# A two-layer encoder on one core: later loads of job blocks, sums written over the raw blocks, six part buffers, A22's low part by VectorE, and the mixer's jobs in another order

## The chip, the cores and the metric

The kernel runs on one core of a Trainium2 chip. The metric is the device time of one execution in microseconds, the median of several runs. The engines are named as in the profile: PE is TensorE's matmul, PEld its weight load, DVE is VectorE, ACT is ScalarE, POOL is GpSimd and SP is SyncE, which here only issues loads.

## The reference

The input is one sequence of 512 tokens with 1024 channels, and each of two layers does this (cut):

```python
h = rmsnorm(x, g_ffn1[l]);  x = x + 0.5 * (silu(h @ w1_a) * (h @ w3_a)) @ w2_a     # 1024 -> 2816 -> 1024
h = rmsnorm(x, g_mix[l]);   p = h @ w_in[l]                                        # fourier|B|C|v|pool|3 gates
y_f = fourier_mix(p_f, w_fourier);  y_c = (B * conv3(C * v)) @ w_conv_out
y_p = pool_scale * per_group(centred_mean(u) - u)                                  # windows 2, 4, 8, 16
x = x + (sig(g_f) * y_f + sig(g_c) * y_c + sig(g_p) * y_p) @ w_o
h = rmsnorm(x, g_ffn2[l]);  x = x + 0.5 * (silu(h @ w1_b) * (h @ w3_b)) @ w2_b
```

After the layers comes a last rmsnorm. All of it is float32.

## The kernel before

**Products.** Activations lie with channels on the 128 partitions and the 512 tokens along the row. A matrix product keeps float32's precision by splitting both operands into a high part (a cast to fp32r) and a low part (the operand minus its high part): `mm` issues three matmuls, high by high (L367), high by low (L368) and low by high (L369).

**Jobs.** The pair w3 and w1 of an f-block of 128 channels (or two blocks of w_in in the mixer) is one *job* in Strassen's form in Winograd's variant. Its weights are cut in four blocks A11, A12, A21, A22, its activations in four quarters, and seven products M1 to M7 take the place of eight. One product is four `mm` of 128x256, so 12 matmuls, and a job has 84. `run` issues per job M1, M5, then M4 of the job before, M6, M3 of the job before, M2, M7. M1, M6, M7 and M4 of one job add up in one PSUM bank; after M1, M6 and M7 ScalarE copies the running sum to a tile sM (`kept`, L536), so M4 can't begin until the copy after M7 has been made. VectorE adds these copies into the two outputs a and b; in a feed-forward stage it then multiplies b by silu(a) (L442 `b<-b,a`), ScalarE casts the high part gh (L354), and VectorE makes the low part gl. The plain tiles, 128x512 matmuls, are w2, w_o, the small maps and the first f-blocks of each feed-forward stage: three (`LEAD`), four in the first stage. `lead` does those while the norm's factor and the split operands n of the jobs (`operands`, four calls a stage) are still being made.

**The stream of weights.** `Weights` loads blocks from DRAM by SP (L193) into 3 buffers `raw` (A11 and A12, 512 KB), 2 of `z` (A21, 256 KB) and 2 of `w22` (A22, 256 KB). Four splitting steps per job fill buffers of parts: *raw* splits the raw block, *sums* makes z + w22 (L236) and that less A11 (L237) and splits both, *rest* makes A11|A12 less the z block (L243, into a tile s34 of its own) and splits it, and *last* splits A22 for M4. Splitting comes in two ways. `parts` casts the high part on ScalarE (L199) and subtracts on VectorE (L200). `added_parts` writes minus the block on ScalarE (L212), lets POOL issue a DMA that adds the block from DRAM to it once more (L213), and casts the high part (L214); VectorE has no part in it. *raw* and *last* use this way, so the low part of A22 costs ScalarE one pass and POOL one DMA.

**What sets the order.** A planner logs every tile and product in the order in which PE needs them with a rough time, and subtracts from it a number per kind of step (`AHEAD`, in planner's microseconds). A step is written into the program once PE's place has come that near, if its buffers are free. After that the framework's scheduler puts each engine's instructions in their order; at run time each engine works its list strictly in order, and waits at an instruction whose inputs or whose buffer aren't there. SP too issues one load after the other, and a load waits for the release of its buffer. A w22 buffer is free when the steps *sums* and *last* have read it.

## Time and profile before

| | us |
|---|---|
| median of 3 runs | 2104.84 (2100.64 to 2105.34) |
| the profiled execution | 2107.87 |
| its span in the trace | 2106.1 |
| PE busy in the span | 2049.9 |
| DVE busy | 1288.2 |
| ACT busy | 1214.6 |
| POOL busy | 383.4 |

The mean granted clock of TensorE was 0.993 of 2.4 GHz in the profiled execution. The run goes in this order: the first feed-forward stage with its lead (0 to about 398 us of the trace), the mixer of the first layer (398 to 662), the second feed-forward stage (662 to 1036) and the third (1036 to 1430), the mixer of the second layer (1430 to 1700), and the last stage. A matmul's record shows a longer time than the next one's distance, because matmuls overlap: the pace is the distance of their starts. Idle time before an instruction stands in brackets behind it, with what ended it.

### The profile page before, as it was taken

What the parts mean: (1) busy time and instruction counts of PE and PEld (TensorE: products, weight loads), DVE (VectorE), ACT (ScalarE), POOL (GpSimd) and SP (SyncE); (2) the same over time, 40 slices, a digit from 0 to 9 for tenths busy, and PEclk for the clock granted to TensorE, in tenths of its full rate; (3) what the DMA queues carried; (4) which work ended last, traced back from release to release, by engine and by line L of the source; (5) the groups of instructions that cost most, each with busy time, mean ns of one, the idle gap of its engine ahead of it and who ended that gap; (6) DMA issues with size and microseconds to landing.
All of it is one profiled execution on the core that took longest, in us unless ns stands there. A gap on an engine that the chain in (4) does not pass through costs nothing. (4 is left out here: it accounts for less than half of the span.)

```text
span 2106.1 us, 34329 instructions
## 1 busy us (share of the span) xinstructions
PE 2049.9 (97%) x13590; PEld 1870.8 (89%) x13590; DVE 1288.2 (61%) x1868; ACT 1214.6 (58%) x1963; POOL 383.4 (18%) x452
## 2 busy tenths in 40 slices
PE   8899999999999999999999999999999999999998
PEld 6798998899988899899889899988999888988996
DVE  4863674698876575366366546638888656653653
ACT  5762764776655665366466446548666556644652
POOL 3310111211221310011231001122122123100100
PEclk9999999999999999999999999999999999999999
DMA  8763774877665776477567557658777567744751
GB/s 232 164 178 95 173 177 130 171 169 175 159 161 150 154 188 163 105 172 182 137 135 188 145 125 165 181 124 162 175 174 180 141 156 151 181 141 113 173 152 54
DMA packets 121555, 329.03 MB, mean 156 GB/s; under 512 B 13489, under 2 KB 15153, under 8 KB 121393
## 3 DMA queue, kind: packets, MB, share of 16 engines
q0 software_dynamic: 45360, 121.28, 34.2%
q1 hardware_dynamic: 75888, 205.31, 30.0%
q8 instruction: 106, 1.74, 0.3%
q14 instruction: 57, 0.46, 0.1%
q10 hardware_dynamic: 144, 0.24, 0.0%
HBM read 312.10 MB, written 2.10 MB: 149 GB/s over the span
## 5 line engine op out<-in xcount | busy, mean ns | idle before, releaser
L368 PE MATMUL ps<-n,parth 128*128 128x256 f32 x2760 | 777.9, 282 | 9.2 <-DMA n<-t 4.6
L369 PE MATMUL ps<-n,partl 128*128 128x256 f32 x2760 | 777.2, 282 | 8.2 <-DMA partl<-weights 5.4
L367 PE MATMUL ps<-n,parth 128*128 128x256 f32 x2760 | 777.2, 282 | 7.7 <-ACT n L484 2.4
L368 PEld LDWEIGHTS ps<-n,parth 128*128 128x128 f32 x2760 | 522.2, 189 | 12.7 <-DMA n<-t 5.8
L367 PEld LDWEIGHTS ps<-n,parth 128*128 128x128 f32 x2760 | 521.8, 189 | 12.2 <-ACT n L484 2.8
L369 PEld LDWEIGHTS ps<-n,partl 128*128 128x128 f32 x2760 | 522.0, 189 | 10.0 <-DMA partl<-weights 6.5
L213 POOL DMA_DIRECT2D partl<-weights x152 | 133.9, 881 | 631.3 <-ACT partl L212 523.0
L367 PE MATMUL ps<-gh,parth 128*128 128x512 f32 x616 | 242.9, 394 | 0.0
L368 PE MATMUL ps<-gl,parth 128*128 128x512 f32 x616 | 242.6, 394 | 0.0
L369 PE MATMUL ps<-gh,partl 128*128 128x512 f32 x616 | 242.5, 394 | 0.0
L200 DVE TENSOR_TENSOR partl<-z,parth 128x1024 fp32r<-128x1024 f32 x115 | 142.8, 1242 | 153.0 <-ACT parth L199 151.3
L213 POOL DMA_DIRECT2D part22l<-weights x115 | 101.1, 879 | 726.3 <-ACT a L662 418.6
L199 ACT CAST parth<-raw 128x1024 fp32r<-128x1024 f32 (+3 forms) x127 | 125.2, 986 | 174.4 <-PE ps L368 123.2
L200 DVE TENSOR_TENSOR partl<-raw,parth 128x1024 fp32r<-128x1024 f32 (+3 forms) x127 | 152.1, 1203 | 113.5 <-ACT parth L199 113.1
L214 ACT CAST parth<-raw 128x1024 fp32r<-128x1024 f32 (+1 forms) x152 | 157.8, 1038 | 90.6 <-PE ps L368 60.7
L212 ACT ACTIVATE partl<-raw 128x1024 fp32r<-128x1024 f32 (+1 forms) x152 | 158.7, 1044 | 14.6 <-DMA raw<-weights 10.3
L200 DVE TENSOR_TENSOR partl<-s,parth 128x1024 fp32r<-128x1024 f32 x115 | 145.8, 1268 | 34.2 <-ACT parth L199 34.0
L236 DVE TENSOR_TENSOR z<-z,w 128x512 f32<-128x512 f32 x115 | 80.2, 697 | 127.1 <-DMA w<-weights 116.1
L199 ACT CAST parth<-z 128x1024 fp32r<-128x1024 f32 x115 | 120.4, 1047 | 51.6 <-PE ps L368 48.9
L536 ACT COPY sM<-ps 128x256 f32<-128x256 f32 x345 | 121.5, 370 | 47.6 <-PE ps L369 46.0
L367 PE MATMUL ps<-n,part22h 128*128 128x256 f32 x460 | 134.0, 291 | 11.1 <-ACT sM L536 10.3
L243 DVE TENSOR_TENSOR s<-raw,z 128x1024 f32<-128x1024 f32 x115 | 141.5, 1231 | 1.0
(184 smaller groups left out, 3539.9 us busy)
## 6 DMA issues: line engine op xcount, KB each, us to landing
raw<-weights SPq DMA_DIRECT2D x258, 512.0 KB, 4.1
partl<-weights POOLq DMA_DIRECT2D x145, 512.0 KB, 6.2
z<-weights SPq DMA_DIRECT2D x115, 256.0 KB, 4.1
w<-weights SPq DMA_DIRECT2D x115, 256.0 KB, 4.1
part22l<-weights POOLq DMA_DIRECT2D x115, 256.0 KB, 5.3
n<-t POOLq DMA_DIRECT2D x48, 256.0 KB, 5.4
x<-x_t SPq DMA_DIRECT2D x8, 256.0 KB, 5.4
raw<-weights SPq DMA_DIRECT2D x11, 128.0 KB, 3.5
```

The source lines that it names most:

```text
L199: self.nc.scalar.copy(hi[:, :w], src)
L200: self.tail.append((self.t, self.made, lambda: self.nc.vector.tensor_tensor(out=lo[:, :w], in0=src, in1=hi[:, :w].bitcast(F32), op=ALU.sub ...
L212: self.nc.scalar.activation(lo[:, :w], src, AF.Copy, scale=-1.0)
L213: self.nc.gpsimd.dma_start(lo[:, :w], self.source(key), accum_op=ALU.add)
L214: self.nc.scalar.copy(hi[:, :w], src)
L236: v.tensor_tensor(out=z[:, 2 * S :], in0=z[:, :S], in1=w22, op=ALU.add)
L243: v.tensor_tensor(out=s34, in0=raws.pop(("first", key))[:, : 2 * S], in1=raws.pop(("third", key))[:, : 2 * S], op=ALU.subtract,)
L367: nc.tensor.matmul(ps, ah, bh, start=start, stop=False, skip_group_check=more)
L368: nc.tensor.matmul(ps, ah, bl, start=False, stop=False, skip_group_check=more)
L369: nc.tensor.matmul(ps, al, bh, start=False, stop=stop, skip_group_check=more)
L536: nc.scalar.copy(b["s" + q], ps)
```

## The change

- **Plan.** Loads of A11|A12 begin 21 (before 24) planner's microseconds ahead, loads of A21 and A22 17 (19); the steps *raw*, *sums* and *rest* are made one earlier (14, 9, 8), *last* 8 ahead instead of 12. Six part buffers for five; the tile s34 is gone, and UNITS, the activation tiles, fall from 50 to 48.
- ***rest*** writes its difference over the raw block, which so stays taken until the split has read it.
- ***last*** uses `parts`: 115 ScalarE passes (L212, 128x512) and 115 accumulating DMAs of 256 KB go, and 115 subtractions of 128x512 on VectorE come.
- **operands** makes two separate tiles of its two inputs, writes them contiguously, and gives M1 the 256-wide pair whose casts are first; three small subtractions become four.
- **The first lead** asks for the norm's factor at its step 12 (15), for the spread at 14 (17), for the four operands at 15, 17, 20, 23 (18, 21, 25, 28).
- **HALF** is 10 for 11: the first stretch of jobs of a feed-forward stage is one shorter, the second one longer.
- **Mixer.** After the Fourier gates come pool, conv, b and p jobs interleaved; before, two pool jobs stood among the Fourier gates. In the pool gates the sum onto yf moves from POOL to VectorE (16 additions of 128x512), and the tiles z and y of the convolution come from the activations' pool.

```diff
-LEAD, HALF = 3, 11
+LEAD, HALF = 3, 10
-    AHEAD = {... "load1": 24.0, "load2": 19.0, "raw": 13.0, "sums": 8.0, "rest": 7.0, "last": 12.0}
+    AHEAD = {... "load1": 21.0, "load2": 17.0, "raw": 14.0, "sums": 9.0, "rest": 8.0, "last": 8.0}
-    BUFS = {"raw": 3, "z": 2, "w22": 2, "s34": 1, "part": 5, "part22": 1}
+    BUFS = {"raw": 3, "z": 2, "w22": 2, "part": 6, "part22": 1}
...
-            s34 = self.tile_of("s34", 2 * S)
-            v.tensor_tensor(
-                out=s34, in0=raws.pop(("first", key))[:, : 2 * S], in1=raws.pop(("third", key))[:, : 2 * S],
...
+            raw = raws.pop(("first", key))[:, : 2 * S]
+            v.tensor_tensor(out=raw, in0=raw, in1=raws.pop(("third", key))[:, : 2 * S], op=ALU.subtract)
+            self.ready["rest", key] = self.parts(raw)
...
-            self.ready["last", key] = self.added_parts(raws.pop(("fourth", key)), ("fourth", key), S, "part22")
+            self.ready["last", key] = self.parts(raws.pop(("fourth", key)), S, "part22")
...
-        place = {"M1": (0, 0), "M2": (0, 1), "M3": (3, 0), "M5": (1, 0), "M7": (1, 1), "M6": (2, 0), "M4": (2, 1)}
+        place = {"M1": (3, 0), "M2": (0, 0), "M3": (0, 1), "M5": (1, 0), "M7": (1, 1), "M6": (2, 0), "M4": (2, 1)}
...
-            at = {"factor": 15, "spread": 17, "operands": (18, 21, 25, 28), "done": (24, 26, 29, 99)}
+            at = {"factor": 12, "spread": 14, "operands": (15, 17, 20, 23), "done": (26, 29, 99)}
...
-            if i in (1, 2):
-                job("pool", 2 * i - 2, OFF_P + (2 * i - 2) * P, OFF_P + (2 * i - 1) * P)
...
+        for do, i in (
+            (pool_in, 0), (conv_in, 0), (pool_in, 2), (pool_gate, 0), (conv_in, 1), (conv_gate, 0), (pool_gate, 1),
+            (conv_in, 2), (pool_gate, 2), (conv_in, 3), (conv_gate, 2), (pool_gate, 3),
+        ):
+            do(i)
...
-                ptt(yf[m], yf[m], s, ALU.add)
+                tt(yf[m], yf[m], s, ALU.add)
```

How the change moves instructions shows at three places. The first is VectorE's list in the steady part of a feed-forward stage, one job's round; the numbers behind the names are buffers of single allocations. Before:

```order
L236 TENSOR_TENSOR z_13249<-z_13249,w22_13251 128x512
L442 TENSOR_TENSOR b_13194<-b_13194,a_13193 128x512
L442 TENSOR_TENSOR b_13327<-ps_13286,sM1_13211 128x256
L237 TENSOR_TENSOR z_13249<-z_13249,raw_13155 128x512
L200 TENSOR_TENSOR partl_13380<-s34_13377,parth_13379 128x1024
L442 TENSOR_TENSOR gl_13310<-b_13194,gh_13309 128x512
L442 TENSOR_TENSOR a_13326<-ps_13214,sM7_13323 128x256
L243 TENSOR_TENSOR s34_13510<-raw_13155,z_13249 128x1024
L200 TENSOR_TENSOR partl_13405<-z_13249,parth_13404 128x1024
L442 TENSOR_TENSOR b_13327<-ps_13214,sM6_13265 128x256
```

Now the same round on VectorE, with L228, L229, L235 and L192 for L236, L237, L243 and L200:

```order
L192 TENSOR_TENSOR part22l_13392<-w22_13132,part22h_13391 128x512
L431 TENSOR_TENSOR b_13316<-ps_13207,sM6_13255 128x256
L431 TENSOR_TENSOR b_13316<-b_13316,a_13315 128x512
L228 TENSOR_TENSOR z_13389<-z_13389,w22_13394 128x512
L431 TENSOR_TENSOR b_13447<-ps_13408,sM1_13335 128x256
L192 TENSOR_TENSOR partl_13472<-raw_13190,parth_13471 128x1024
L431 TENSOR_TENSOR gl_13430<-b_13316,gh_13429 128x512
L431 TENSOR_TENSOR a_13446<-ps_13338,sM7_13443 128x256
L229 TENSOR_TENSOR z_13389<-z_13389,raw_13321 128x512
L235 TENSOR_TENSOR raw_13321<-raw_13321,z_13389 128x1024
L192 TENSOR_TENSOR partl_13490<-z_13389,parth_13489 128x1024
```

The product b by a stood behind the addition that reads w22 and now stands ahead of it. New is part22l three places ahead of that addition, and the two hang together: the slot of w22_13132, which part22l reads last, is the one into which w22_13394 is loaded.

The second place is SP's list of loads in the same stretch, before:

```order
L193 DMA raw_13288<-weights 128x1024
L193 DMA w22_13118<-weights 128x512
L193 DMA z_13249<-weights 128x512
L193 DMA raw_13421<-weights 128x1024
L193 DMA w22_13251<-weights 128x512
L193 DMA z_13382<-weights 128x512
```

And now:

```order
L185 DMA raw_13059<-weights 128x1024
L185 DMA z_13127<-weights 128x512
L185 DMA w22_13001<-weights 128x512
L185 DMA raw_13190<-weights 128x1024
L185 DMA z_13258<-weights 128x512
L185 DMA w22_13132<-weights 128x512
```

The load of w22 stood right behind a raw block of 512 KB; now the 256 KB of z stand between.

The third place is VectorE's list in the first lead, from the norm's spread on, before:

```order
L470 SCALAR_TENSOR_TENSOR s34_381<-x0_86,cst_70,rstd_373 128x2x256
L470 SCALAR_TENSOR_TENSOR s34_381<-x1_87,cst_70,rstd_373 128x512
L442 TENSOR_TENSOR t_382<-s34_381 128x512
L237 TENSOR_TENSOR z_527<-z_527,raw_423 128x512
L442 TENSOR_TENSOR t_383<-s34_381,t_382 128x256
```

And now:

```order
L457 SCALAR_TENSOR_TENSOR t_357<-x0_86,cst_70,rstd_345 128x512
L457 SCALAR_TENSOR_TENSOR t_358<-x1_87,cst_70,rstd_345 128x512
L431 TENSOR_TENSOR t_359<-t_357 128x256
L431 TENSOR_TENSOR t_359<-t_358,t_357 128x256
L431 TENSOR_TENSOR t_360<-t_358,t_359 128x256
L431 TENSOR_TENSOR t_360<-t_358,t_360 128x256
L229 TENSOR_TENSOR z_560<-z_560,raw_493 128x512
```

The subtraction that reads the raw block stood in the middle of the first operand's four steps, and now stands behind all of them.

## Rows read from the trace of the kernel before

**Rows 1.** The page, busy time, share of the span and instructions of PE

```profile
PE 2049.9 (97%) x13590; PEld 1870.8 (89%) x13590; DVE 1288.2 (61%) x1868; ACT 1214.6 (58%) x1963; POOL 383.4 (18%) x452
```

**Rows 2.** Waits of PEld, whole run: us in total, times, longest us

```profile
PEld ps L367 <- ACT sM L536: 18.6, 35, 3.1
PEld ps L369 <- DMA partl<-weights: 7.7, 6, 2.6
PEld ps L368 <- DMA n<-t: 5.8, 6, 1.6
...
PEld ps L369 <- DMA part22l<-weights: 4.0, 5, 1.9
```

**Rows 3.** Timeline of PE, 26 matmuls apart: start us, us, engine, instruction

```profile
1809.79 0.28 PE L369 MATMUL ps<-n,partl 128*128 128x256 f32 x1
...
1812.86 0.28 PE L368 MATMUL ps<-n,parth 128*128 128x256 f32 x1
```

**Rows 4.** Chain of waits, 1955 to 1986 us: start us, us, what

```profile
1959.13 4.18 DMA w<-weights
...
1969.33 4.25 DMA w<-weights
```

**Rows 5.** Timeline of SP's queue, just ahead of the load in Rows 4

```profile
1958.70 0.33 SPq L193 DMA_DIRECT2D raw<-weights  x1
```

**Rows 6.** The tile w, 808 to 815 us, one load, issued at 811.9

```profile
DMA to landing us min/median/max: 2.7/2.7/2.7
```

**Rows 7.** Timeline of DVE, one job's round

```profile
1964.61 0.42 DVE L442 TENSOR_TENSOR b<-ps,sM 128x256 f32<-128x256 f32 x1
1964.95 0.68 DVE L237 TENSOR_TENSOR z<-z,raw 128x512 f32<-128x512 f32 x1
1965.55 1.22 DVE L200 TENSOR_TENSOR partl<-s,parth 128x1024 fp32r<-128x1024 f32 x1
1966.68 0.69 DVE L442 TENSOR_TENSOR gl<-b,gh 128x512 fp32r<-128x512 f32 x1
```

**Rows 8.** Groups of DVE by form: busy us, mean ns | idle before, releasers

```profile
L236 DVE TENSOR_TENSOR z<-z,w 128x512 f32<-128x512 f32 x115 | 80.2, 697 | 127.1 <-DMA w<-weights 116.1 <-issue 8.1 <-DMA z<-weights 2.8
```

**Rows 9.** Timeline of DVE, one of the longer of these waits

```profile
1817.04 0.69 DVE L236 TENSOR_TENSOR z<-z,w 128x512 f32<-128x512 f32 x1 [4.48 <-DMA w<-weights]
```

**Rows 10.** Busy time by windows: us, PE, PEld, DVE, ACT, POOL, PEclk, DMA share, GB/s

```profile
64.80:71.60 6.80, 4.24 (x18) 3.95 (x19) 6.09 (x9) 3.50 (x7) 3.96 (x4) 0.50 0.90 153
...
1819.20:1822.60 3.40, 3.29 (x15) 3.29 (x16) 3.27 (x5) 1.24 (x4) 0.00 (x0) 0.51 0.03 6
```

**Rows 11.** Busy time by windows, the first mixer

```profile
398.00:662.00 264.00, 257.62 (x1963) 247.21 (x1962) 209.68 (x339) 178.98 (x305) 54.73 (x78) 0.99 0.71 167
```

**Rows 12.** Timeline of POOL in the first mixer

```profile
594.81 1.29 POOL L445 TENSOR_TENSOR yf<-yf,a 128x512 f32<-128x512 f32 x1 [0.65 <-DVE a L968]
596.04 0.89 POOL L213 DMA_DIRECT2D partl<-weights  x1
598.37 2.19 POOL L445 TENSOR_TENSOR yf<-yf,b 128x512 f32<-128x512 f32 x1 [1.43 <-DVE b L968]
```

**Rows 13.** Timeline of DVE at the same place

```profile
599.66 1.98 DVE L200 TENSOR_TENSOR partl<-raw,parth 128x1024 fp32r<-128x1024 f32 x1
```

**Rows 14.** Timeline of PE, first lead, eight matmuls apart

```profile
36.74 0.40 PE L367 MATMUL ps<-hh,parth 128*128 128x512 f32 x1
...
38.60 0.39 PE L369 MATMUL ps<-hh,partl 128*128 128x512 f32 x1
```

**Rows 15.** Timeline of DVE, first lead

```profile
49.20 0.69 DVE L237 TENSOR_TENSOR z<-z,raw 128x512 f32<-128x512 f32 x1 [4.09 <-DMA raw<-weights]
```

**Rows 16.** Timeline of PE, the first jobs

```profile
64.80 0.57 PE L367 MATMUL ps<-n,parth 128*128 128x256 f32 x1 [2.05 <-ACT n L484]
67.93 0.58 PE L368 MATMUL ps<-n,parth 128*128 128x256 f32 x1 [2.56 <-DVE n L442]
```

**Rows 17.** DMA queues on the page: packets, MB, share of 16 engines; q0 is POOL's

```profile
q0 software_dynamic: 45360, 121.28, 34.2%
```

More of the change, by code (lines that the diff above doesn't have):

```diff
@@ L32 @@
 AW = 516
-UNITS = 50
-LEAD, HALF = 3, 11
+UNITS = 48
+LEAD, HALF = 3, 10
 WARM = 10
@@ L71, in start @@
         pass
-    def keep(self, *tags):
-        pass
-    give = keep
     def tile(self, spec, share=1.0, added=False):
@@ L97 @@
 class Layout:
-    AHEAD = {"load": 21.0, "tile": 10.0, "added": 13.0, "load1": 24.0, "load2": 19.0, "raw": 13.0, "sums": 8.0,
-             "rest": 7.0, "last": 12.0}
+    AHEAD = {"load": 21.0, "tile": 10.0, "added": 13.0, "load1": 21.0, "load2": 17.0, "raw": 14.0, "sums": 9.0,
+             "rest": 8.0, "last": 8.0}
     def __init__(self, log):
@@ L176, in give @@
             self.used[t] -= 1
-    def keep(self, *tags):
-        assert self.take(*tags)
     def source(self, key):
@@ L239, in step @@
         elif kind == "rest":
-            if not self.take("part", "s34"):
+            if not self.take("part"):
                 return False
-            s34 = self.tile_of("s34", 2 * S)
-            v.tensor_tensor(
-                out=s34, in0=raws.pop(("first", key))[:, : 2 * S], in1=raws.pop(("third", key))[:, : 2 * S],
-                op=ALU.subtract,
-            )
-            self.ready["rest", key] = self.parts(s34)
-            self.give("raw", "z", "s34")
+            raw = raws.pop(("first", key))[:, : 2 * S]
+            v.tensor_tensor(out=raw, in0=raw, in1=raws.pop(("third", key))[:, : 2 * S], op=ALU.subtract)
+            self.ready["rest", key] = self.parts(raw)
+            self.give("raw", "z")
         elif kind == "last":
@@ L463, in operands @@
     def operands(j):
[L466 to L469 removed]
+        w1, w2, z1, z2 = (act.tile([P, AW], F32, tag="act", name="t")[:, :S] for _ in range(4))
+        for odd, w in enumerate((w1, w2)):
             nc.vector.scalar_tensor_tensor(
[L471 to L479 removed]
+                out=w, in0=x[2 * j + odd], scalar=state["gain"][2 * j + odd], in1=state["r"],
+                op0=ALU.mult, op1=ALU.mult,
+            )
+        left, right = slice(0, Q), slice(Q, S)
+        tt(z1[:, left], w1[:, right], w1[:, left], ALU.subtract)
+        tt(z1[:, right], w2[:, right], w1[:, right], ALU.subtract)
+        tt(z2[:, left], w2[:, right], z1[:, left], ALU.subtract)
+        tt(z2[:, right], w2[:, left], z2[:, left], ALU.subtract)
         units = [act.tile([P, AW], F32R, tag="act", name="n")[:, :S] for _ in range(7)]
         pairs = [units[0:2], units[2:4], units[4:6], (units[6][:, :Q], units[6][:, Q:])]
[L482 to L483 removed]
+        sources = [w2, z1, z2, w1[:, left]]
+        for i in (3, 0):
             nc.scalar.copy(pairs[i][0], sources[i])
@@ L489, in operands @@
             nc.scalar.copy(pairs[i][0], sources[i])
-        for i in (0, 3):
+        for i in (3, 0):
             tt(pairs[i][1], sources[i], pairs[i][0].bitcast(F32), ALU.subtract)
-        place = {"M1": (0, 0), "M2": (0, 1), "M3": (3, 0), "M5": (1, 0), "M7": (1, 1), "M6": (2, 0), "M4": (2, 1)}
+        place = {"M1": (3, 0), "M2": (0, 0), "M3": (0, 1), "M5": (1, 0), "M7": (1, 1), "M6": (2, 0), "M4": (2, 1)}
         ops = {q: cut(pairs[i], h * Q, (h + 1) * Q) for q, (i, h) in place.items()}
@@ L620, in lead @@
                     normed(k + 2, "g_ffn1", 0)
-                for i in range(2 * k - 2, 2 * k):
+                for i in range(3 * k - 3, 3 * k):
                     if 0 <= i < KD:
                         squares(i)
-            if n == 2:
-                weights.keep("s34")
             if n == at["factor"]:
@@ L638, in lead @@
                 spec = (w + s, l, k * P, f * P, P)
-                mm(ps, weights.tile(spec, added=not first or n >= 15), h[k], k == 0, k == KD - 1)
+                mm(ps, weights.tile(spec, added=not first or n >= 12), h[k], k == 0, k == KD - 1)
         for i in sorted(pss):
@@ L835, in mix @@
         pss = [psum() for _ in range(NT)]
-        weights.keep("s34")
         pf = []
```

31 lines of the change are left out of this document (6 added, 25 removed).

## The prediction

> **What bounds the kernel now.** I read the shares of the engines first, then what PE's weight loads wait for, then the chain of waits at the longest of these waits. PE is busy for 97% of the span [rows 1], and its matmuls keep one pace: the two of [rows 3] stand 3.07 us and 26 matmuls apart, 0.118 us each, so the 84 of a job take 9.92 us. The change leaves their number as it is. What can be won is therefore only what PE waits, and what the half clock costs behind a wait. The waits' largest row is M4, which can't begin before ScalarE has copied the sum after M7: 18.6 us in 35 waits [rows 2]. Behind it are DMAs that POOL issues, 7.7 us for parts, 5.8 us for the operands n and 4.0 us for A22's low part [rows 2].
>
> The chain shows why the copy is late. A load of w22 starts at 1959.13 and takes 4.18 us, the next one starts at 1969.33 [rows 4]: a loop of 10.2 us a job, against PE's 9.92. The links are, in the program's order: ScalarE splits A22 after PE's M4, which frees the slot; SP loads the next w22 into it; VectorE's L236, which reads it, waits; behind L236 in VectorE's list stands b by a, behind that on ScalarE the cast gh, and behind gh the copy that M4 needs. VectorE stood idle at L236 for 116.1 us [rows 8], in one of the longer cases 4.48 us [rows 9]; there PE stood too, and then ran at a granted clock of 0.51, the lower of its two levels (1.2 and 2.4 GHz), for 3.4 us [rows 10]. The load is slow for what stands ahead of it on SP, a raw block of 512 KB issued 0.43 us earlier [rows 5]; one with no raw block ahead landed in 2.7 us [rows 6].
>
> **The change part by part.**
>
> *The loop in the feed-forward stages.* The order moves b by a ahead of the addition that reads w22, so gh and the copy of M7's sum no longer stand behind a load. That takes the cause out of M4's waits. But a new loop lies wholly on VectorE: part22l reads the old w22 last, its slot takes the new one, and the addition that needs it comes three places later. So VectorE idles for most of each landing. One round is the landing L plus the work from that addition to part22l. By starts, a 256-wide step takes 0.34 us (1964.61 to 1964.95), a 512-wide one 0.60 and a 1024-wide one 1.13 [rows 7]. Four 512-wide (the addition, gl, the subtraction of A11, part22l) make 2.40, three 1024-wide 3.39, two 256-wide 0.68: 6.47 us. The other two steps lie under the landing. For L the bounds are 2.7 us, alone [rows 6], and 4.2 us, behind 512 KB [rows 4]. With 256 KB of z ahead, I take 3.0, below the middle, since z is released a step before part22l and so goes out about 0.6 us ahead, where the raw block was 0.43 us ahead. The round is then 9.5 us, under PE's 9.92; the point where VectorE becomes the bound is L = 9.92 - 6.47 = 3.45 us. ScalarE loses 115 passes and is not the bound. Taken: M4's waits 18.6 us, less the 5.6 that I leave for those whose copy is late for other reasons (a busy ScalarE, the first job of a stretch): -13, between -18.6 and, if L stays under 3.45, 0.
>
> *A22's low part by VectorE.* 115 subtractions of 0.60 us are 69 us more on VectorE; they are in the round above and cost nothing by themselves where PE is ahead. The waits for the DMA of part22l, 4.0 us [rows 2], go; since ScalarE's cast follows M4 of the job before, the low part is ready some 7 us ahead of its use (a round less the wait and two steps, an estimate). Both that and the next part count in the mixers.
>
> *The mixers.* POOL's queue is short by the part22l issues and the additions onto yf. At 594.81 such an addition held it for 1.2 us and the DMA of parts behind it began at 596.04 [rows 12]; PE's six waits for such parts are 7.7 us, the longest 2.6 [rows 2]. Gain, with the waits for part22l: up to 11.7, if all of them lie in the mixers. Against it stands VectorE's load: in the first mixer 209.68 of 264 us [rows 11], and there come 16 x 0.60 for A22 and 8 x 0.60 for yf [rows 7], 224 us or 85%, and on top the landings it must wait through, up to 2 us in each of 16 jobs: 224 + 32 is 256 of 264. It just fits on the average, but not in each job, so the waits for VectorE's parts grow. Taken: -4 for both mixers, between -12 and +10 (each mixer 5 us behind, two or three landings that nothing hides).
>
> Here the trace shows something that could make the moved additions cheaper: the addition onto yf that took 2.19 us [rows 12], and the subtraction beside it on VectorE, 1.98 us where the like took 1.22 [rows 7, 13]. The Trainium skill (SBUF — State Buffer, "SBUF: two separate sides") says that VectorE with two SBUF inputs and a GpSimd instruction that reads SBUF take one shared port pair in turn, the loser blocked for the whole time. The trace agrees with a block of some 0.76 us; by that rule each second addition gives VectorE back 0.76 of the 0.60 that it costs, 3 us a mixer, and the term would be -5 instead of -4.
>
> *The first lead.* Factor, spread and operands come three steps earlier. A step is six matmuls of 0.232 us (eight in 1.86 us [rows 14]), so 1.39 us and 4.2 in all. What it can shorten are the waits for the operands when the jobs begin, 2.05 us at 64.80 and 2.56 at 67.93 [rows 16], and the half clock between, 6.8 us at 0.50 [rows 10], which costs 3.4. VectorE's wait for a raw block at 49.20, 4.09 us long [rows 15], stood in the middle of the first operand; it now stands behind it. The two DMAs that each operand issues on POOL move with it; POOL is not full there (3.96 of 6.80 us [rows 10]). The fourth small subtraction costs nothing, two 256-wide for one 512-wide [rows 7]. Taken: -4, half of these 8, between -8 and 0 (if ScalarE's and POOL's work for these operands is only pushed together).
>
> *The later leads.* M1 now needs only the 256-wide pair, which one cast and one subtraction make, and the DMAs are for M5 and later. Of the waits for n, 5.8 us [rows 2], and of the copies before: -3, between -6 and 0.
>
> *The half clock* after waits that go: a stretch of 3.4 us costs 1.7 [rows 10], and one of the later ones goes, or two: -2, between -3.4 and 0. HALF, the buffers and UNITS I cost at nothing: they move which job stands where, and PE's queue of plain tiles covers it; without that cover a job's first parts would be late once a stretch, which the ends above hold.
>
> *Sum:* -13 - 4 - 4 - 3 - 2 = -26 on the profiled execution, 2107.87, gives 2081.9. That execution stands 3.0 above the median of the runs shown, so the median to expect is 2079.
>
> **The rivals.**
>
> *A, no change.* The mixers cost what the feed-forward stages gain. For it: 256 of 264 us on VectorE; against it: VectorE ran ahead of PE in the other half of the time. The mixers' end, +10, half of M4's gain, the two leads, and no clock: 10 - 6.5 - 4 - 3 = -3.5, 2101 on the median. Decided by VectorE's idle time in the mixer.
>
> *B, slower.* The new loop on VectorE is the bound. At L = 4.2, the round is 10.7 us, 0.8 a job behind PE. The parts are planned 8 to 9 us ahead and some 5 us of that can be used up; a stretch of twelve jobs falls 9.6 - 5 = 4.6 us behind, one of seven about 0.6, so the four feed-forward stages lose 21, the mixers, with more on VectorE a job, 6 each, 12. With the gains elsewhere (-4, -3, -13): +13, and 2118 on the median. It decides at L = 3.45, and is slower than now by more than the gains from about 4.0. For it: z goes out just ahead of w22. Against: half the bytes of the raw block.
>
> *C, the start doesn't do what the step numbers say:* the factor's chain goes through POOL and ScalarE, whose work lies there anyway, and the first lead gains nothing: 2083.
>
> *D, the relief of the DMAs reaches further.* POOL's queue took 34.2% of the 16 engines' time for 121 MB [rows 17]; the 115 accumulations of 256 KB are 30 MB, a quarter, 8 points. If all landings get faster, the waits for parts and n (7.7 + 5.8) go entirely, 13.5, of which the terms above count 7; with two stretches of half clock that is some 10 more, 2069. Against it: the load of [rows 6] landed in 2.7 us though an accumulation ran beside it. The Trainium skill (DMA: Bandwidth & Descriptors, "Issuing engines are not separate DMA queues") says that transfers of all issuing engines interleave on the same 16; D is what follows from it here, and the row speaks for the order of SP's queue instead.
>
> **How the numbers follow.** The forecast, 2064 to 2098, has 0.57, C 0.10, D 0.08, A 0.12, B 0.13. About 0.3%, 6.3 us, is what a measurement of this kernel can tell from no change: faster is under 2098.5, slower over 2111. The first three are faster, A the same, B slower: 0.75, 0.12, 0.13. The range goes from 2062 to 2110, which leaves out B and a few hundredths below.
>
> **What would show it.** If the loop is right, the waits of M4 for ScalarE's copy nearly go, VectorE's wait at the addition that reads w22 stays, at 2 to 3 us in most jobs, the load lands in 2.6 to 3.4 us, and loads of w22 follow each other at PE's 9.9 us. If the landing is near 4.2 and PE waits for VectorE's parts late in the long stretches, B is right. If these waits stand in the mixers alone, A. The first jobs should begin without half a clock; if they still wait for n at about the same distance behind the factor, C. In the mixers no wait for POOL's DMA of parts should be left. What makes the prediction wrong is a wait that VectorE's longer list opens where the trace of before shows none.

## The result and the profile after

The changed kernel takes 2078.85 us (median of 4 runs, 2076.94 to 2079.62) against 2104.24 for the kernel before in the same comparison: a ratio of 0.9881, with a 95% interval of 0.9864 to 0.9898. The forecast of 2079 came true, on the side and at the size forecast. The experiments below show that this sum is right although some of its terms are not: the feed-forward stages gained more than forecast, one term has the wrong sign and one came to nothing, and one edit alone gives more than the whole change.

The span falls from 2106.1 to 2077.3 us. On the page of the changed kernel PE is 16.7 us less busy than in [rows 1], VectorE 68.9 us busier. The 115 subtractions account for that: in e6 below, which adds only them, VectorE is 73.9 us busier than in the kernel before.

```profile
PE 2033.2 (98%) x13590; PEld 1865.7 (90%) x13590; DVE 1357.1 (65%) x2022; ACT 1175.1 (57%) x1847; POOL 266.2 (13%) x321
```

What PE's weight loads wait for in the changed kernel, whole run (us in total, times, longest; L356 to L358 are the lines L367 to L369 of before):

```profile
PEld ps L356 <- ACT pfh L825: 8.1, 2, 4.0
PEld ps L357 <- DMA n<-t: 7.2, 6, 1.7
PEld ps L357 <- DVE n L431: 7.0, 4, 2.3
PEld ps L356 <- ACT half L859: 6.1, 2, 3.1
PEld ps L356 <- ACT parth L191: 4.2, 3, 3.3
...
PEld ps L356 <- ACT sM L523: 2.2, 2, 1.5
...
PEld ps L358 <- DMA partl<-weights: 2.0, 1, 2.0
```

Against [rows 2], the waits for ScalarE's copy sM fall from 18.6 to 2.2 us, both of them in the first job and none at M4. The waits for POOL's DMA of parts fall from 7.7 to 2.0, those for part22l from 4.0 to none. Grown to the top are the waits for pfh and for the Fourier halves, one of each per mixer: 8.1 and 6.1 us, where the kernel before had 3.4 and 1.1.

The loop around w22, in a steady stretch of the changed kernel: SP's queue, then ScalarE's cast, then VectorE (start us, us, instruction, idle before):

```profile
1243.12 0.33 SPq L185 DMA_DIRECT2D w<-weights  x1
1248.56 0.33 SPq L185 DMA_DIRECT2D raw<-weights  x1
1252.48 0.33 SPq L185 DMA_DIRECT2D z<-weights  x1
1253.09 0.33 SPq L185 DMA_DIRECT2D w<-weights  x1
```

```profile
1251.67 0.62 ACT L191 CAST part22h<-w 128x512 fp32r<-128x512 f32 x1 [0.53 <-PE ps L357]
```

```profile
1252.37 0.68 DVE L192 TENSOR_TENSOR part22l<-w,part22h 128x512 fp32r<-128x512 f32 x1
...
1255.76 0.69 DVE L228 TENSOR_TENSOR z<-z,w 128x512 f32<-128x512 f32 x1
```

Two loads of w22 are 9.97 us apart, where [rows 4] had 10.2; the raw block goes out 4.5 us ahead of w22 instead of 0.43 [rows 5]; and ScalarE waits for PE before the cast, so PE sets the pace and not the loop. Over all the feed-forward stages the middle distance of two loads of w22 is 9.92 us, where it was 10.20 before (worked out from the issue times in the traces). The page's list of DMA issues gives the landing of w22 in the middle of all 115 loads (KB each, us), of before and then of after:

```profile
w<-weights SPq DMA_DIRECT2D x115, 256.0 KB, 4.1
```

```profile
w<-weights SPq DMA_DIRECT2D x115, 256.0 KB, 2.8
```

Where the time went can be read from the starts of PE's matmuls, since both programs have 13,590 of them and their stages have the same counts. Worked out from the traces' start times, in us between two matmuls by number; each column is one execution:

```
from .. to matmul, stage              before   after   e6      e9      e10     e8
0 .. 300      first lead, first jobs   82.3     79.4    79.3    80.2    80.5    75.3
300 .. 2389   first FFN              322.5   319.8   319.5   319.8   320.2   319.6
2389 .. 2450  first mixer begins       11.1    17.4    10.7    10.7    19.2    16.2
2450 .. 4640  first mixer, rest       317.7   311.7   313.9   311.7   313.7   311.9
4640 .. 4700  lead                      9.1    11.0     8.9     7.9    12.4    10.8
4700 .. 6935  second FFN              345.8   340.2   340.9   340.8   342.8   340.0
6935 .. 7000  lead                     13.1    12.9    13.1    12.8     9.9    15.3
7000 .. 9181  third FFN               336.7   329.9   329.4   330.5   330.5   329.8
9181 .. 9240  second mixer begins      10.5    16.6    10.5    10.9    18.5    15.8
9240 .. 11440 second mixer, rest      325.1   312.3   316.5   312.7   317.9   312.3
11440 .. 11500 lead                     9.0    11.0     8.7     8.6    11.9    11.1
11500 .. 13580 last FFN               312.3   304.5   304.3   304.7   304.7   305.7
```

After less before: the start -2.9, the feed-forward stages -23.0, the rest of the mixers -18.8, their beginnings +12.3, the later leads +3.7; together -28.7 of the span's -28.8. A gain of 45 us was made and 16 us were given back at four short places, the mixers' beginnings and two of the later leads. e6 alone, which has the old mixer, shows -12.4 of the -18.8 in the rest of the mixers, and e9, which adds the new mixer to it, -18.4.

What holds PE at the beginning of the first mixer, ScalarE's list and then PE's:

```profile
403.65 2.41 ACT L825 ACTIVATE pfh<-ps,rtok 128x512 fp32r<-128x512 f32 x4
...
412.81 1.06 ACT L204 ACTIVATE partl<-raw 128x1024 fp32r<-128x1024 f32 x1 [2.88 <-PE ps L357]
```

```profile
404.38 0.58 PE L356 MATMUL ps<-parth,pfh 128*128 128x260 f32 x1 [3.61 <-ACT pfh L825]
415.74 0.39 PE L356 MATMUL ps<-n,parth 128*128 128x256 f32 x1 [2.85 <-ACT half L859]
```

The copies pfh stand behind casts for the operands that came late, and the copies of the halves behind a pass for a later job's parts, which itself waits 2.88 us until PE gives a part buffer back. From within the first of these waits the clock is at its lower level (1.2 GHz) for 6.8 us (columns: us, PE, PEld, DVE, ACT, POOL, PEclk, DMA share, GB/s):

```profile
403.00:409.80 6.80, 5.42 (x24) 5.35 (x25) 6.80 (x12) 5.33 (x10) 0.89 (x1) 0.50 0.74 159
```

### The profile page after: what moved, and what is told of

It is laid out like the page before. It is cut to its first block, busy times and chain, and to the rows that moved or that the text cites. A ratio compares the mean times of both kernels' runs of the same rounds, so it can differ in the third digit from the quotient of the medians.

```text
span 2077.3 us, 33989 instructions
## 1 busy us (share of the span) xinstructions
PE 2033.2 (98%) x13590; PEld 1865.7 (90%) x13590; DVE 1357.1 (65%) x2022; ACT 1175.1 (57%) x1847; POOL 266.2 (13%) x321
## 4 chain that ended last, share of the span: by engine, by line
PE 88%; DVE 3%; DMA 3%; ACT 2%; issue 2%; POOL 1%; POOLq 0%; SPq 0%; ACTq 0%; DVEq 0%
PE ps L356 29%; PE ps L357 29%; PE ps L358 29%; DMA raw<-weights 1%; DVE t L457 1%; DVE t L431 1%; DMA n<-t 1%; ACT parth L206 0%; DMA w<-weights 0%; DMA z<-weights 0%; POOL n L474 0%; ACT n L476 0%; DVE raw L235 0%; POOL a L434 0%; DVE n L431 0%
## 5 line engine op out<-in xcount | busy, mean ns | idle before, releaser
L356 PE MATMUL ps<-n,parth 128*128 128x256 f32 x2760 | 776.7, 282 | 10.1 <-ACT half L859 5.7
L358 PE MATMUL ps<-n,partl 128*128 128x256 f32 x2760 | 775.9, 281 | 0.0
L356 PEld LDWEIGHTS ps<-n,parth 128*128 128x128 f32 x2760 | 521.4, 189 | 13.1 <-ACT half L859 6.1
L358 PEld LDWEIGHTS ps<-n,partl 128*128 128x128 f32 x2760 | 523.0, 189 | 0.0
L192 DVE TENSOR_TENSOR partl<-raw,parth 128x1024 fp32r<-128x1024 f32 (+2 forms) x241 | 285.0, 1186 | 104.8 <-ACT parth L191 104.8
L191 ACT CAST parth<-raw 128x1024 fp32r<-128x1024 f32 (+2 forms) x241 | 243.9, 1013 | 171.5 <-PE ps L357 146.1
L356 PE MATMUL ps<-gh,parth 128*128 128x512 f32 x608 | 239.7, 394 | 0.0
L358 PE MATMUL ps<-gh,partl 128*128 128x512 f32 x608 | 239.5, 394 | 0.0
L523 ACT COPY sM<-ps 128x256 f32<-128x256 f32 x345 | 127.5, 370 | 143.9 <-PE ps L358 142.9
L204 ACT ACTIVATE partl<-raw 128x1024 fp32r<-128x1024 f32 (+1 forms) x152 | 159.6, 1050 | 11.1 <-PE ps L357 7.2
L192 DVE TENSOR_TENSOR partl<-z,parth 128x1024 fp32r<-128x1024 f32 x115 | 140.2, 1219 | 32.8 <-ACT parth L191 32.8
L431 DVE TENSOR_TENSOR b<-ps,sM 128x256 f32<-128x256 f32 x222 | 93.2, 420 | 98.9 <-PE ps L358 98.7
L235 DVE TENSOR_TENSOR raw<-raw,z 128x1024 f32<-128x1024 f32 x115 | 140.7, 1223 | 20.7 <-ACT partl L204 13.6
L191 ACT CAST part22h<-w 128x512 fp32r<-128x512 f32 x115 | 71.3, 620 | 128.0 <-PE ps L357 112.0
L358 PEld LDWEIGHTS ps<-gh,partl 128*128 128x128 f32 x608 | 114.1, 188 | 26.9
L356 PEld LDWEIGHTS ps<-gh,parth 128*128 128x128 f32 x608 | 114.2, 188 | 25.6
```

Of the source, the lines that this page charges most:

```text
L191: self.nc.scalar.copy(hi[:, :w], src)
L192: self.tail.append((self.t, self.made, lambda: self.nc.vector.tensor_tensor(out=lo[:, :w], in0=src, in1=hi[:, :w].bitcast(F32), op=ALU.sub ...
L204: self.nc.scalar.activation(lo[:, :w], src, AF.Copy, scale=-1.0)
L235: v.tensor_tensor(out=raw, in0=raw, in1=raws.pop(("third", key))[:, : 2 * S], op=ALU.subtract)
L356: nc.tensor.matmul(ps, ah, bh, start=start, stop=False, skip_group_check=more)
L358: nc.tensor.matmul(ps, al, bh, start=False, stop=stop, skip_group_check=more)
```

## The experiments

Three comparisons of four kernels each were made, each with its own runs of the kernel before (medians 2104.89, 2101.57 and 2099.75 us), so kernels of different comparisons are compared by their ratios to it. The changed kernel's ratio is 0.9881 (0.9864 to 0.9898).

**e1, five part buffers in the changed kernel.**

```diff
-    BUFS = {"raw": 3, "z": 2, "w22": 2, "part": 6, "part22": 1}
+    BUFS = {"raw": 3, "z": 2, "w22": 2, "part": 5, "part22": 1}
```

> The changed kernel with five part buffers instead of six, nothing else. On VectorE the product b by a then stands behind the addition that reads w22 again in 49 of the jobs, and on SP the load of w22 stands right behind a raw block again (83 of 115). Theory 1, the order around w22 is what the feed-forward stages gained by: the waits of M4 for ScalarE's copy come back, 12 to 20 us in all, and the time is 2092 to 2102. Theory 2, the gain comes from A22's low part on VectorE and the accumulating DMAs that are gone: the time stays under 2085. Theory 3, the sixth buffer helps by itself in the mixers only: waits for parts there grow and M4's stay away.

Measured: 2087.6 us, ratio 0.9914 (0.9897 to 0.993). b by a stands behind the addition that reads w22, and still M4 doesn't wait (PEld's row for sM, the whole run):

```profile
PEld ps L356 <- ACT sM L523: 0.4, 1, 0.4
```

SP and VectorE in a steady round of this kernel:

```profile
1940.17 0.33 SPq L185 DMA_DIRECT2D raw<-weights  x1
1944.12 0.33 SPq L185 DMA_DIRECT2D w<-weights  x1
```

```profile
1947.60 0.69 DVE L228 TENSOR_TENSOR z<-z,w 128x512 f32<-128x512 f32 x1 [0.79 <-DMA w<-weights]
1948.21 0.68 DVE L431 TENSOR_TENSOR b<-b,a 128x512 f32<-128x512 f32 x1
```

Theory 1 falls, and the time lies 2.6 us above theory 2's. The raw block stands right ahead of w22 in SP's list as before, but in time it goes out 3.95 us earlier. Which instruction stands where on VectorE is not what took M4's waits away; the time of the raw load might be. The sixth buffer is worth about 0.3%, at the edge of what the two intervals tell apart; the row that grows without it is PE's wait for the operands' DMAs, 13.7 us for 7.2.

**e2, A22's low part by POOL's DMA in the changed kernel.** The step *last* by `added_parts`, 12 ahead:

```diff
-            self.ready["last", key] = self.parts(raws.pop(("fourth", key)), S, "part22")
+            self.ready["last", key] = self.added_parts(raws.pop(("fourth", key)), ("fourth", key), S, "part22")
```

> The changed kernel with A22's low part by ScalarE, POOL and an accumulating DMA as before (and that step 12 ahead as before). On VectorE b by a still stands ahead of the addition that reads w22. Theory 1: M4's waits for ScalarE's copy stay near nothing in the feed-forward stages, the waits for POOL's DMAs of parts and of A22's low part come back in the mixers (4 to 10 us), VectorE gains 69 us of free time that PE doesn't need: 2080 to 2090. Theory 2 (A22 on VectorE is the gain): M4's waits come back too and the time is over 2092.

Measured: 2083.7 us, ratio 0.9899 (0.9878 to 0.9921). The waits for sM come back in a small way:

```profile
PEld ps L356 <- ACT sM L523: 6.8, 10, 1.5
```

Of these, 2.5 us stand at the start, much as in the changed kernel, and 4.3 us in eight waits of at most 0.8 us behind it, against 18.6 us in the kernel before. The waits for A22's low part and for POOL's parts do not come back. The time lies in theory 1's range and can't be told from that of the changed kernel. So neither the sixth buffer nor A22 on VectorE is needed alone to take most of M4's waits away; something else in the change is enough.

**e3, the loads of job blocks as early as before, in the changed kernel.**

```diff
-    AHEAD = {... "load1": 21.0, "load2": 17.0 ...
+    AHEAD = {... "load1": 24.0, "load2": 19.0 ...
```

> The changed kernel with the loads of job blocks as early as before (24 and 19 planner's microseconds instead of 21 and 17). Ahead of the mixer VectorE stood 4.24 us at a subtraction that waits for a raw block, and the operands' work and ScalarE's copies pfh were late behind it: PE waits 4.0 us there in each mixer. Theory 1, the later loads cost that: the waits for pfh fall from 8.1 us to under 4, the time falls by 4 to 8 us to 2071 to 2075. Theory 2, the raw block waits for its buffer, not for the plan's number: nothing moves, 2077 to 2081. Theory 3, the order of SP's queue suffers elsewhere: slower by 3 us or more.

Measured: 2076.97 us, ratio 0.9871 (0.9851 to 0.9892), not told apart from the changed kernel. The waits for pfh go from 8.1 to 6.7 us only, so theory 1 is a miss: the plan's number for the loads is not what makes the mixers begin late.

**e4, the eight copies of the Fourier halves by VectorE, in the changed kernel.**

```diff
-                nc.scalar.copy(half, ps)
+                nc.vector.tensor_copy(half, ps)
```

> The changed kernel with the eight copies of the Fourier halves out of PSUM by VectorE instead of ScalarE. In the changed kernel they stand on ScalarE behind a pass that waits 2.88 us for a part buffer, PE waits 3.1 and 3.0 us for a bank, and the clock is halved after it, in each mixer. Theory 1, a queue's head is what holds them: the waits go, and the time falls by 5 to 9 us (6 us of waits and two stretches of half clock of 1.7 each), 2070 to 2074. Theory 2, PE waits later for the same buffer or the same operands: under 2 us are gained. Theory 3: VectorE, at 84% in the mixer, passes the delay on: no gain or slower.

Measured: 2084.32 us, ratio 0.9897 (0.988 to 0.9914): no gain. The waits for the halves do go, and the first mixer's beginning (matmuls 2389 to 2450) takes 12.6 us instead of 17.4. But the rest of that mixer takes 315.8 instead of 311.7. PE's row for the operands' DMAs doubles from 7.2:

```profile
PEld ps L357 <- DMA n<-t: 15.3, 9, 3.4
```

That fits theory 2: the last operand is late behind the same wait of ScalarE for a part buffer, its DMA is issued at 412.98 (414.88 in the changed kernel), and PE, which reaches the first jobs 4.3 us earlier, meets it there. That VectorE passes on a delay of its own (theory 3) is not ruled out.

**e5, rest over the raw block in the kernel before, nothing else.**

```diff
-            if not self.take("part", "s34"):
+            if not self.take("part"):
                 return False
-            s34 = self.tile_of("s34", 2 * S)
...
+            raw = raws.pop(("first", key))[:, : 2 * S]
+            v.tensor_tensor(out=raw, in0=raw, in1=raws.pop(("third", key))[:, : 2 * S], op=ALU.subtract)
+            self.ready["rest", key] = self.parts(raw)
+            self.give("raw", "z")
```

> The kernel before with one part of the change: the step rest writes over the raw block, and no tile s34 is taken for it. The raw block is then released by the split that reads it, and in the run with five part buffers that put SP's load of the raw block 4 us ahead of the load of w22, where it was 0.43 us ahead in the kernel before, though it stood right in front of it in the list in both. Theory 1, this is what took away M4's waits: they fall from 18.6 us to under 6, the landing of w22 from 4.2 to 2.6 to 3.4 us, and the time is 2085 to 2096. Theory 2, A22's low part on VectorE did it: M4's waits stay over 12 us and the time at 2100 to 2108.

Measured: 2089.72 us, ratio 0.9934 (0.9909 to 0.996). M4's waits fall to 1.6 us. SP and POOL in a steady round, and the landing of w22 between 1910 and 1970 us:

```profile
1948.92 0.33 SPq L193 DMA_DIRECT2D raw<-weights  x1
1952.65 0.33 SPq L193 DMA_DIRECT2D w<-weights  x1
```

```profile
1953.03 0.88 POOL L213 DMA_DIRECT2D part22l<-weights  x1 [5.40 <-ACT a L659]
```

```profile
DMA to landing us min/median/max: 2.5/2.7/3.6
```

The raw block is now released by the split that reads it, not by the subtraction, and SP's load of it has moved from 0.43 to 3.73 us ahead of w22. The accumulation for A22 still starts 0.38 us behind w22's load and doesn't keep it from landing in 2.7 us. Over the feed-forward stages the loads of w22 are now 9.95 us apart (10.20 before). Theory 1 holds. The gain in the feed-forward stages is partly given back: PE waits 16.9 us for pfh as the mixers begin, in four waits, the longest 8.2.

**e6, A22's low part by VectorE in the kernel before** (`parts` in *last*, and that step 8 ahead for 12; nothing else):

```diff
-            self.ready["last", key] = self.added_parts(raws.pop(("fourth", key)), ("fourth", key), S, "part22")
+            self.ready["last", key] = self.parts(raws.pop(("fourth", key)), S, "part22")
```

> The kernel before with the other part: A22's low part by VectorE, that step 8 ahead. Theory 1 (the raw block's release is the cause): the raw load still goes out right ahead of w22, M4's waits stay over 10 us; the accumulations and the waits for them go, 2 to 8 us: 2096 to 2103. Theory 2 (A22 on VectorE is the cause): M4's waits fall under 6 us, 2083 to 2093.

Measured: 2067.46 us, ratio 0.9828 (0.98 to 0.9855). This one edit is faster than the whole change. In M4's waits theory 2 holds too, they are 1.1 us; the time lies 16 us below its range, since the mixers' beginnings stay as short as before (10.7 and 10.5 us in the table, 18.5 and 18.6 in e5). What the step's later place in the plan does by itself was not run. The raw block still goes out close ahead of w22. SP, ScalarE and VectorE in a steady round, and the landing of w22 between 1900 and 1960 us:

```profile
1930.37 0.33 SPq L193 DMA_DIRECT2D raw<-weights  x1
1931.63 0.33 SPq L193 DMA_DIRECT2D w<-weights  x1
```

```profile
1930.26 0.62 ACT L199 CAST part22h<-w 128x512 fp32r<-128x512 f32 x1 [0.64 <-PE ps L368]
```

```profile
1934.73 0.69 DVE L236 TENSOR_TENSOR z<-z,w 128x512 f32<-128x512 f32 x1 [0.40 <-DMA w<-weights]
...
1938.94 1.22 DVE L243 TENSOR_TENSOR s<-raw,z 128x1024 f32<-128x1024 f32 x1
```

```profile
DMA to landing us min/median/max: 2.5/3.0/3.1
```

These rows and those of before give one reading for e5 and e6. In the kernel before the round closes so, on VectorE, SP and ScalarE:

```profile
1963.40 0.69 DVE L236 TENSOR_TENSOR z<-z,w 128x512 f32<-128x512 f32 x1 [1.60 <-DMA w<-weights]
1967.62 1.21 DVE L243 TENSOR_TENSOR s<-raw,z 128x1024 f32<-128x1024 f32 x1
```

```profile
1968.90 0.33 SPq L193 DMA_DIRECT2D raw<-weights  x1
1969.33 0.38 SPq L193 DMA_DIRECT2D w<-weights  x1
```

```profile
1968.57 0.63 ACT L212 ACTIVATE part22l<-w 128x512 fp32r<-128x512 f32 x1
```

VectorE's L243 ends and frees the raw block, SP loads it and w22 behind it, L236 waits for w22, and from there VectorE works until L243 ends again. From the raw load's issue to the landing of w22 it is 0.43 + 4.18 = 4.61 us [rows 4, 5]; from L236's start to the end of L243 it is 1968.83 - 1963.40 = 5.43 us. With some 0.15 between, the round is 10.2 us, what [rows 4] shows, against PE's 9.92. A second path closes at the same moment: ScalarE's pass L212, which reads the old w22 last, ends at 1969.20, when SP has just issued the raw load. The profile's chain of waits goes over ScalarE; which of the two really holds the load of w22 can't be told from so small a difference, but both run through its landing. In e6 the pass L212 is gone and the first piece is 1.26 + 3.0 = 4.26 us, so the round would be 9.8 us: just under PE's pace, and ScalarE waits for PE (0.64 us) instead. In e5 the raw block is out of that piece. The loop lay only 0.3 us above PE's pace, so that either edit was enough: over the feed-forward stages the loads of w22 are 9.92 us apart in e6. That the two loads together are 0.35 us faster here because the accumulations are gone fits the Trainium skill (DMA: Bandwidth & Descriptors, "Issuing engines are not separate DMA queues"), by which POOL's transfers run on the same engines as SP's. The traces separate this from the later issue of w22: of the loads in the feed-forward stages that go out less than 0.6 us behind a raw block, the middle one lands in 4.25 us in the kernel before (42 loads) and in 3.60 us in e6 (13 loads), where no accumulation for A22 runs beside them.

**e7, the tile s34 back in the changed kernel, and five part buffers.**

```diff
+            s34 = self.tile_of("s34", 2 * S)
...
-    BUFS = {"raw": 3, "z": 2, "w22": 2, "part": 6, "part22": 1}
+    BUFS = {"raw": 3, "z": 2, "w22": 2, "s34": 1, "part": 5, "part22": 1}
```

> The changed kernel with the tile s34 for rest again and, since the space is then gone, five part buffers; all else as changed. Against the run with five part buffers and rest in place (2087.6) only the place of the difference is other. Theory 1: the raw load goes out right ahead of w22 again, M4's waits come back, 8 to 16 us, 2094 to 2104. Theory 2: no more than 3 us away from 2087.6.

Measured: 2091.38 us, ratio 0.9941 (0.9919 to 0.9963). M4's waits don't come back as theory 1 had it (5.0 us of sM waits in 4, half of it one wait at the start), which fits e6, since A22 is on VectorE here. The time is below theory 1's range and further from e1 than theory 2 allowed, but its ratio can't be told apart from e1's 0.9914. In the feed-forward stages the loads of w22 stay 9.90 us apart. Against e6 (0.9828) it has the change's plan, operands, first lead, HALF and mixer, and 1.1% more time, with 9.3 us of waits for pfh (3.4 in e6) and 9.1 for the halves (2.2). So the cost of the beginnings is in these parts.

**e8, the first lead's steps as before, in the changed kernel** (cut; with them two more lines of the first lead go back: the squares are made two a step for three, and the weights come by `added_parts` from step 15 on for 12).

```diff
-            at = {"factor": 12, "spread": 14, "operands": (15, 17, 20, 23), "done": (26, 29, 99)}
+            at = {"factor": 15, "spread": 17, "operands": (18, 21, 25, 28), "done": (24, 26, 29, 99)}
```

> The changed kernel with the first lead's steps as before (factor 15, spread 17, operands 18, 21, 25, 28). In the changed kernel the first jobs wait nearly as long as before, PE is 2.9 us earlier at its matmul 300. Theory 1, the earlier steps gave these: 3 to 5 us slower, 2082 to 2084. Theory 2, they gave nothing, the raw load and ScalarE's queue decide: 2077 to 2081.

Measured: 2075.94 us, ratio 0.9866 (0.9842 to 0.9891). Both theories are wrong about the place: PE reaches its matmul 300 at 76.5 us, 4.1 earlier than in the changed kernel. The whole time can't be told from the changed kernel's. The earlier steps gave nothing, and in this trace they cost 4 us at the start; the start's gain came from the other edits. e6, with the old steps, already has 3.0 us of it.

**e9, the kernel of e6 with the change's mixer** (order of jobs, the additions onto yf by VectorE, z and y in the activations' pool).

> The kernel before with A22's low part by VectorE (as in the run that gave 2067.5) and with the change's mixer: its order of jobs, the addition onto yf by VectorE, z and y in the activations' pool. Plan, buffers, the tile s34, operands, the first lead and HALF as before. PE's time from its matmul 2450 to 4640 and from 9240 to 11440 is 311.7 and 312.3 us in the changed kernel, 313.9 and 316.5 in the run with A22 alone. Theory 1, the change's mixer gives these 6 us and they add up: 2059 to 2063, faster than both kernels. Theory 2, they came from the sixth part buffer or the plan: 2065 to 2069.

Measured: 2066.14 us, ratio 0.9827 (0.9802 to 0.9851), the fastest kernel here and faster than both kernels of this case, but not told apart from e6. In the table the mixers' rests take 2.2 and 3.8 us less than in e6, yet the measurement doesn't confirm a gain of 6 us.

**e10, the kernel of e9 with the change's operands** (separate tiles w1 and w2 of the activations' pool, M1 on the 256-wide pair, no share in s34).

```diff
-        w = wpool.tile([P, 2 * S], F32, tag="s34", bufs=1, name="s34")
+        w1, w2, z1, z2 = (act.tile([P, AW], F32, tag="act", name="t")[:, :S] for _ in range(4))
...
-            if n == 2:
-                weights.keep("s34")
...
-        weights.give("s34")
```

> As the run before, and with the change's operands (contiguous, M1 on the pair cast first, no share in s34). Theory 1, this is what makes the later leads slow (about 2 us more each from PE's matmul 4640 to 4700 and 11440 to 11500, and waits for DVE n): 3 to 8 us slower than the run before. Theory 2, the slow leads and the waits for pfh come from rest in place and the later plan: within 2 us of the run before, or up to 4 us faster by the first jobs, which begin earlier in the kernel that had these operands with the old steps (matmul 300 at 76.5 us against 80.5).

Measured: 2088.93 us, ratio 0.993 (0.9908 to 0.9953): 1% slower than e9 by this edit alone, far more than theory 1 expected. It shows at theory 1's places and, most of all, at the mixers' beginnings: these take 19.2 and 18.5 us (10.7 and 10.9 in e9), two of the later leads 12.4 and 11.9 (7.9 and 8.6), the third 9.9 (12.8). The profiled executions exaggerate: e10's is the slowest of its six and e9's the fastest of its four, 30.7 us apart by their spans where the medians are 22.8 apart. Some 12 us of the 30.7 are the clock, which is at its lower level for 44.4 us in e10 and 20.4 in e9, not counting the runs' ends. ScalarE at the first mixer's beginning, in e9 and then in e10:

```profile
409.94 2.30 ACT L877 COPY half<-ps 128x260 f32<-128x260 f32 x8
412.07 1.13 ACT L199 CAST parth<-s 128x1024 fp32r<-128x1024 f32 x1
```

```profile
408.69 1.04 ACT L199 CAST parth<-s 128x1024 fp32r<-128x1024 f32 x1 [0.40 <-PE ps L369]
...
414.11 1.05 ACT L199 CAST parth<-z 128x1024 fp32r<-128x1024 f32 x1 [3.79 <-PE ps L369]
...
417.97 2.29 ACT L870 COPY half<-ps 128x260 f32<-128x260 f32 x8
```

And PE's waits in e10:

```profile
PEld ps L367 <- ACT half L870: 9.1, 2, 4.6
PEld ps L367 <- ACT pfh L836: 7.9, 4, 3.5
```

The operands used to hold the tile s34 (`weights.keep`) until the last of them was made, and the step *rest* needs that tile. So in e9 the splits of the job's sums stand behind the operands' casts and the copies of the halves. In e10 nothing holds them back: they are written in among the operands, and one of them waits 3.79 us at the head of ScalarE's list for a part buffer, with the last operand's casts and the copies of the halves behind it. That the old operands cost 1% less is shown. That the reservation is the reason, and not the layout of the new tiles, was not run by itself, but e5 speaks for it: there the operands are the old ones, only *rest* no longer needs the tile they hold, and the mixers' beginnings take 18.5 and 18.6 us. The three kernels in which *rest* has to wait for the operands' tile (before, e6, e9) take 10.5 to 11.1 us there; all others take 15 to 20, but e4, which moved the copies themselves.

**e11, the additions onto yf by POOL, in the changed kernel.**

```diff
-                tt(yf[m], yf[m], s, ALU.add)
+                ptt(yf[m], yf[m], s, ALU.add)
```

> The changed kernel with the additions onto yf on POOL as before. My reason for the mixers said that POOL's queue, held by these additions and by A22's DMAs, made PE wait for parts. Theory 1, the additions alone still hold it: waits for DMA of parts come back, 2 to 5 us, 2081 to 2085. Theory 2, with A22's DMAs gone POOL has room: within 2 us of 2078.9, VectorE saves 11 us that nobody waits for.

Measured: 2078.6 us, ratio 0.9885 (0.9865 to 0.9906), the same as the changed kernel; theory 2.

**e12, the mixer's jobs in the old order, in the changed kernel** (the list of twelve steps replaced by the old loops).

> The changed kernel with the mixer's jobs in the order of the kernel before. Theory 1, the order gave the mixers their gain (up to 6 us): 2081 to 2087, with waits for VectorE's parts or ScalarE's in the middle of the mixer. Theory 2, the order gave nothing, POOL's relief did: 2077 to 2081.

Measured: 2076.2 us, ratio 0.9877 (0.9856 to 0.9897), the same, as theory 2 has it for the order. Neither the mixer's order nor its additions (e11) move the time; that POOL's relief did it, the other half of theory 2, isn't shown.

## Why the prediction was right, and where it was not

**The feed-forward stages, -13 forecast and -2 for the clock.** They gave -23.0. M4's waits went, as forecast, and with them some 7 us of shorter delays, each under 0.15 us, that the table of waits hardly shows (both read from the starts of the matmuls: 15.8 us in longer gaps and 9.2 in shorter ones before, none and 1.9 after). The landing of 3.0 us that I took was close (2.8). The step that failed is the reason given first, that the order moves b by a ahead of the addition that reads w22: in the round of e1 shown it stands behind it, and M4 doesn't wait. What counted is the time from the raw load to the landing of w22. The prediction had named that load as the cause of the slow landing and put z in between as the cure; it did not look at the time at which the raw block is released. The accumulations, which e6 shows to slow a load that close behind a raw block by 0.65 us, it left out of this term, going by [rows 6], where no raw block was near.

**The loop on VectorE** of 9.5 us, decided at a landing of 3.45, was built without what follows PE on VectorE's list: the sums that it adds, and the cast of A22, which comes after PE's M4. With them VectorE can't run ahead. It idles for PE and for the cast, the loads are 9.97 us apart, and the bound is PE. What VectorE waits for in the changed kernel (us in total, times, longest):

```profile
DVE b L431 <- PE ps L358: 98.7, 75, 4.5
DVE part22l L192 <- ACT part22h L191: 69.0, 56, 3.3
...
DVE z L228 <- DMA w<-weights: 38.1, 46, 8.5
```

So the wait of 2 to 3 us in most jobs at the addition that reads w22, a sign that the prediction named, is a miss: 5 of 115 waits there are 2 us or longer. Rival B's threshold was never tested.

**The mixers, -4.** They gave -6.4, as -18.8 and +12.3. The waits for POOL's parts and for part22l went, as forecast, 9.7 us in all. The -18.8 is no single edit's: by the same count it is -14.2 in e5, -12.4 in e6, and still -16.9 in e2, where A22's DMAs are back on POOL. VectorE's load was under-counted, since a mixer has 20 jobs and not 16 (20 of the 115 casts of A22 in each); with 20, the sum of 256 us would have been 266.5 of 264. But the landings in it, 2 us in each job, were far too many: VectorE's waits for w22 are 38.1 us in the whole run. The +12.3 was in no step: I named the first jobs' operands as faster in every lead, and didn't ask what s34 had kept behind them.

**The first lead, -4.** It gave -2.9, but e8 shows that the earlier steps themselves gave nothing. Rival C describes that part rightly; that the start still came near its term is luck.

**The later leads, -3.** They gave +3.7, the wrong sign. M1 does need less, but what is made first is not what is late: in e10 the new operands cost 4.5 and 3.3 us at two of these leads and give 2.9 at the third.

**The half clock, -2.** It came to nothing. Stretches at the lower level add up to 23.9 us in both traces, not counting the runs' ends: the one behind M4's wait at 1819 went, with two others and half of that at the first jobs, and at the mixers' beginnings there are 17.0 us for 3.4. The first jobs did not begin without half a clock, as the prediction had it as a sign, but with 3.4 us of it.

**Rival A** is right only in that the mixers give back a part of the gain, but they do so at their beginnings and on ScalarE, not by VectorE's load, which rose from 209.68 us [rows 11] to 220.24 in the first mixer without PE waiting for it. **Rival D**: the end of the accumulations sped the loads in e6, but e2, which has the accumulations, can't be told from the changed kernel. The moved additions onto yf, for which the prediction had two prices, made no difference that could be measured (e11).

So the sum came out by luck in its parts: in the traces -23.0 stood for -15, and 16.0 of losses less 18.8 gained in the mixers and 2.9 at the start, -5.7 in all, stood for -11.

## What to carry to other kernels

A wait that repeats every round is a loop: add up its pieces and compare with the pace of the bound engine. Here it was 10.2 us against 9.9, so either edit that took 0.3 us out of it gave 20 to 23 us in the feed-forward stages, and both together gave no more (23.0). A buffer shared by two kinds of work is also an order between them; before it is taken away, ask what it had kept from the head of an in-order queue. And try the edits of a bundle one by one: one step of this one, moved by itself, gave 1.7%, all of it together 1.2%.

## What the runs showed of the hardware

A 256 KB load landed 4.18 us after its issue when a 512 KB load had gone out 0.43 us ahead of it by the same engine, SP, and an accumulating DMA of 256 KB 0.28 us behind it by POOL. Over the feed-forward stages, with the 512 KB less than 0.6 us ahead, the middle landing was 4.25 us with these accumulations (kernel before, 42 loads) and 3.60 us without (e6, 13 loads). With the 512 KB more than 3 us ahead it was 2.68 us with them (e5, 58 loads) and 2.58 us without (e6, 17 loads): there the accumulation, issued 0.38 us behind the load in the round shown, did it no visible harm.
